# An emission-order model that counts VectorE and GpSimd holding each other up at SBUF

## The chip, the core and the metric

The kernel runs on one core of a Trainium2 chip. The metric is the device time of one execution in microseconds (us); lower is better. TensorE (PE) does matmuls and writes to PSUM, VectorE (DVE), ScalarE (ACT) and GpSimd (POOL) do elementwise work, and SyncE (SP) issues the DMA transfers. Each engine works through its own queue of instructions in the order in which the program wrote them, and semaphores hold an instruction until the data it needs are there.

## The reference

One layer of a latent generator in float32, with 1024 latent tokens and 256 context tokens of width 1024:

```
hn   = rms_norm(h) * gain * (1 + scale) + shift          # h = ctx, then x
proj = hn @ w_in                                          # columns: q,k,v | a,b | z | u_pool | z_pool
q, k, v = silu(short_conv(qkv, 5 taps));  q, k = l2_norm(q), l2_norm(k)
o    = gated_delta_rule(q, k, v, g, beta, state)          # 8 heads, both directions, chunked
o    = rms_norm(o_f + o_b) * silu(z)
y    = (box_mean(u_pool) - u_pool) @ pool_w * silu(z_pool) # 4 groups, windows 2, 4, 8, 16
out  = rms_norm(x + gate * (concat(o, y) @ w_out))
```

The context runs first through the same weights; only its final scan states are used, as the start of the scans of x.

## The kernel before

Matmuls of the large projections are done in three passes of split operands: a weight tile `w` is split into `whi` (ACT copies it, rounded) and `wlo` (POOL subtracts `whi`), an input tile into `hnhi` and `hnlo`, and the products hi*hi, lo*hi and hi*lo are added up in one PSUM bank (`gemm_half`).

The program is written out by Python generators. A **main** generator walks over the tiles of the projections: sixteen context tiles (k and v of each head), then for every head of x the tiles v, k, z and q, some tiles of the pooling branch, and in a second pass the pooling tiles and the output projection. Everything else is a **side thread**: `x_sums` and `inputs` (norm, transposition and splitting of x; `x_half`, `x_split`), `conv_post` (the other four taps of the convolution on DVE, then a tanh on ACT, then one more DVE operation), `thread_a` to `thread_s` (the delta rule of one head after another: `stage_a`, `stage_b`, `stage_q`, `stage_s`, `scan_x`), and later `mix_all`, `pool_out`, `load_all` (pooling) and the loads of the output weights.

Which step is written next is decided by the class `Flow`, a model of the engines' time. Its `free` has for each engine the modelled time at which its queue runs empty. `spend` books an instruction: it starts when its engine is free and its operands are there (plus a fixed delay, `AFTER`), and lasts what `Engine.cost` says. For DVE that is 65 + 1.04 ns per element per partition, and 61 more with a per-partition scalar operand; for a POOL `tensor_tensor` 148 + 2.1 ns per element, and 1040 ns where it raises to a power (`power`). So a `scalar_tensor_tensor` of 128x512 on DVE counts as 658 ns, one of 128x256 as 392 ns, a POOL `tensor_tensor` of 128x512 as 1223 ns and of 128x1024 as 2298 ns.

`run` steps the main generator, and before each of its steps every side thread that is due: `due` is the time at which a thread's last operation is finished by the model or, where the thread names an engine that it wants next, not before that engine's queue is within `SLACK` (500 ns) of running empty. A thread is written as soon as the model's PE time has reached its due time. The thread list is in order of priority, `x_sums` and `inputs` first. Flags (`conv`, `k`, `B`, `done`, `mixed`, `pw` and others) let threads and main wait for one another; a flag bears a modelled time.

So the model's numbers are never seen by the chip. They only set in which order the instructions stand in the five queues: a step which the model takes to be ready early is written early, and its engine then waits at that place in the queue if the chip isn't as far.

At the end of the second pass, `load_all` loads and splits the pooling weights of each group (`pwr`, `pw`, flag `pw`), `mix_all` does the box sums on DVE, and `second_half` releases the pool of tiles `poola` once the flag `mixed` is there and puts the tiles of the output projection in its place.

Of the kernel before, what the change touches and what calls it, by code (L numbers as in the profile page):

```python
# [48 lines left out]
GROUPS = (2, 1, 3, 0)  # L49
# [9 lines left out]
PSUM_TAGS = ("mm", "pp", "pa", "sc", "o")  # L59
# [5 lines left out]
}  # L65
ISSUE = 1220.0
LANDED = 950.0


class Flow:  # L70
# [3 lines left out]
    def __init__(self):  # L74
        self.free = dict(pe=0.0, act=0.0, dve=0.0, pool=0.0, sync=0.0)
        self.dma = 0.0
        self.cur = None
        self.flags = {}
        self.sides = []
        self.seen = {}, {}  # L80
        self.slots = {}
        self.stored = 0.0
        self.banks = [0.0, 0.0]


    def born(self, name, place, bufs):
# [15 lines left out]
    def start(self, eng, uses):  # L102
        t = self.free[eng]
        for name, p0, p1, f0, f1, w in uses:
            for v in (1, 0) if w else (1,):
                for (q0, q1, g0, g1, e), end in self.seen[v].get(name, {}).items():
                    if end + 3000.0 > t and q0 < p1 and p0 < q1 and g0 < f1 and f0 < g1:
                        if e == "sync":
                            d = LANDED + (ISSUE if eng == "sync" else 0.0)
                        elif eng == "sync":  # L110
# [15 lines left out]
                            del old[r]  # L126
            self.seen[w].setdefault(name, {})[p0, p1, f0, f1, eng] = end

    def spend(self, eng, ns, uses):
        start = self.start(eng, uses)  # L130
        end = self.free[eng] = start + ns
        self.note(eng, uses, end)
        t = self.cur
        if t is not None:
            t.next = max(t.next, end + NEXT[eng])
            t.last = eng

    def transfer(self, size, uses, load):
# [3 lines left out]
        self.note("sync", uses, end)  # L142
        self.stored = end + LANDED - ISSUE
        t = self.cur
        if t is not None and load:
            t.next = max(t.next, end + LANDED)
            t.held = True
# [166 lines left out]
class Engine:  # L314
# [46 lines left out]
    def __getattr__(self, op):  # L361
        f = getattr(self.real, op)

        def call(*a, **k):
            self.flow.spend(self.name, self.cost(op, a, k), self.uses(op, a, k))
            return f(*a, **k)  # L366

        return call
# [24 lines left out]
def kernel(  # L393
# [23 lines left out]
    pe, act, dve, pool = (Engine(flow, e, n) for e, n in (  # L417
        (nc.tensor, "pe"), (nc.scalar, "act"), (nc.vector, "dve"), (nc.gpsimd, "pool")))
# [225 lines left out]
    def hnx(b, k, t0):  # L644
# [13 lines left out]
                 u=iter([U0 + i * P for i in CH]),  # L658
# [47 lines left out]
    for i, xt in enumerate(xs):  # L706
        sync.dma_start(out=xt, in_=x_d[:, i, :])
        landed.append(flow.dma + LANDED)
    act.activation(out=wab[:, :, 0, :], in_=wab_r, func=ACTF.Copy)
# [886 lines left out]
    start = [ab_gemm(False), next(ctx), next(ctx)]  # L1596
# [180 lines left out]
    def u_back(n):  # L1777
        if n >= NU:
            yield ("up", CH[n - NU])
        sync.dma_start(out=ups[n % NU][:, :, 8:8 + GW], in_=uscr[n].rearrange("p (r w) -> p r w", w=GW))  # L1780
        flow.settle(flow.dma + LANDED)
        flow.flag("u", n)
# [46 lines left out]
    def out_main():  # L1829
# [6 lines left out]
        def free_raw(slot):  # L1836
            free.append(slot)
            flow.flag("rel", released[0])
            released[0] += 1
# [49 lines left out]
        def y_part(t, hf, k0, k1):  # L1889
            hi, lo = ys[t, hf]  # L1890
            load_split(hi[:, k0:k1], lo[:, k0:k1],
                       yscr[hf * KT + k0:hf * KT + k1, :, t * P:(t + 1) * P].rearrange("k p i -> p k i"),
                       "pool", ("y", t, hf, k0))

        def y_tiles(t, hf, al, bufs):
            ys[t, hf] = [al([P, KT, P], f"y{s}", bufs, FP32R) for s in ("hi", "lo")]
# [69 lines left out]
        def ot2(shape, tag, bufs=1, dtype=FP32):  # L1966
            return pools["c"].tile(shape, dtype, tag=tag, name=tag, bufs=bufs)

        def second_half():
            yield ("mixed",)  # L1970
            pl_p.release()
            pools["c"] = Pool(flow, tc.alloc_tile_pool(name="outc", bufs=1, side="right", reuse_waits="tile"))
            wos = {k: [ot2([P, D], f"wo{s}{n}", 1, FP32R) for s in ("hi", "lo")] for n, k in enumerate(KS[:4])}
            yield ("pool", 2)
            for t in range(2):
                y_tiles(t, 1, ot2, 2)
                y_part(t, 1, *PARTS[0])
                wo_load(KS[t], *wos[KS[t]])
            for k in KS[2:4]:
                wo_load(k, *wos[k])  # L1980
            yield ("pool", 3)
            for slot in ("zp0", "zp1"):
                free_raw(slot)
            for t in range(2):
                y_part(t, 1, *PARTS[1])
            for k in KS[4:]:
                wo_load(k, *[pb([P, D], f"d{s}", 4, FP32R) for s in ("hi", "lo")])
            yield ("wo", KS[5])
            closed.update(("zp0", "zp1", "outb"))
            while not closed.issubset(free):  # L1990
                yield ("rel", released[0])
            cols["gate"], cols["fgain"] = gate, fgain = [pb([P, D], "zp", 2) for _ in range(2)]
            sync.dma_start(out=gate, in_=gate_d.partition_broadcast(P))
            sync.dma_start(out=fgain, in_=final_gain.partition_broadcast(P))
            x_load(0)
            x_load(1)
            yield ("heads",)
            y_tiles(2, 1, oa, 3)
            for p in PARTS:
                y_part(2, 1, *p)  # L2000
            y_load(3, 0, oa, 3)
            y_load(3, 1, oa, 3)
# [80 lines left out]
```

## Time and profile before

| what | value |
|---|---|
| time, median of 3 runs | 1300.84 us (1292.27 to 1300.85) |
| the profiled execution | 1300.56 us |
| its span, first to last instruction | 1298.8 us |
| mean granted TensorE clock | 0.97 |
| PE busy | 1202.6 us (93%) |
| DVE busy | 907.3 us (70%) |
| ACT busy | 582.5 us (45%) |
| POOL busy | 413.9 us (32%) |

"Busy" is the time in which an engine has at least one instruction in work. An idle gap is written in brackets with the instruction that ended it. All instructions have one line, 366, because a helper records them; so tiles, not lines, tell them apart. Tile names are written out<-in.

### The profile page before, as it was taken

What the parts mean: (1) busy time and instruction counts of PE and PEld (TensorE: products, weight loads), DVE (VectorE), ACT (ScalarE), POOL (GpSimd) and SP (SyncE); (2) the same over time, 40 slices, a digit from 0 to 9 for tenths busy, and PEclk for the clock granted to TensorE, in tenths of its full rate; (3) what the DMA queues carried; (4) which work ended last, traced back from release to release, by engine and by line L of the source; (5) the groups of instructions that cost most, each with busy time, mean ns of one, the idle gap of its engine ahead of it and who ended that gap; (6) DMA issues with size and microseconds to landing.
All of it is one profiled execution on the core that took longest, in us unless ns stands there. A gap on an engine that the chain in (4) does not pass through costs nothing.

```text
span 1298.8 us, 26423 instructions
## 1 busy us (share of the span) xinstructions
PE 1202.6 (93%) x10631; PEld 965.7 (74%) x10631; DVE 907.3 (70%) x1867; ACT 582.5 (45%) x1514; POOL 413.9 (32%) x447
## 2 busy tenths in 40 slices
PE   8876799899899999999999999999999989799997
PEld 1675667777787887877778778777788767688886
DVE  4798789778885787788886878887334999624212
ACT  2476637544446547464474464643623223322110
POOL 2466433220411413214142232241315544412330
PEclk9887799999998999999999999999999989899999
DMA  9542254223120313112231132212313135664230
GB/s 324 202 114 81 64 150 142 75 58 91 37 49 18 106 46 103 44 52 77 64 104 29 39 102 62 76 49 50 103 52 120 33 122 183 208 206 148 83 112 33
DMA packets 157384, 123.73 MB, mean 95 GB/s; under 512 B 47106, under 2 KB 135115, under 8 KB 157261
## 3 DMA queue, kind: packets, MB, share of 16 engines
q1 hardware_dynamic: 157261, 122.04, 31.1%
q8 instruction: 83, 1.36, 0.4%
q14 instruction: 40, 0.33, 0.1%
HBM read 101.43 MB, written 20.60 MB: 94 GB/s over the span
## 4 chain that ended last, share of the span: by engine, by line
PE 53%; DVE 31%; ACT 7%; DMA 4%; issue 4%; POOL 2%; SPq 0%; DVEq 0%; POOLq 0%; ACTq 0%
PE mm L366 31%; DVE kT L366 7%; PE sc L366 6%; PE o L366 6%; DVE t L366 6%; PE pp L366 5%; PE pa L366 4%; DVE vT L366 4%; DVE ws L366 3%; ACT junk L366 2%; DVE B L366 1%; DVE qT L366 1%; DVE D L366 1%; ACT u L366 1%; ACT ks L366 1%
## 5 line engine op out<-in xcount | busy, mean ns | idle before, releaser
L366 PE MATMUL mm<-hnhi,wlo 128*128 128x512 f32 x768 | 319.2, 416 | 0.0
L366 PE MATMUL mm<-hnhi,whi 128*128 128x512 f32 x768 | 319.1, 416 | 0.0
L366 PE MATMUL mm<-hnlo,whi 128*128 128x512 f32 x768 | 315.9, 411 | 0.0
L366 POOL TENSOR_TENSOR wlo<-wraw,whi 128x512 fp32r<-128x512 f32 x110 | 156.9, 1432 | 401.0 <-ACT whi L366 391.7
L366 PEld LDWEIGHTS mm<-hnhi,wlo 128*128 128x128 f32 x768 | 146.6, 191 | 24.8 <-issue 0.9
L366 PEld LDWEIGHTS mm<-hnhi,whi 128*128 128x128 f32 x768 | 146.9, 191 | 23.9 <-issue 0.9
L366 PEld LDWEIGHTS mm<-hnlo,whi 128*128 128x128 f32 x768 | 147.0, 191 | 22.8
L366 DVE SCALAR_TENSOR_TENSOR kT<-u,cw,kT 128x512 f32<-128x512 f32 (+1 forms) x96 | 100.9, 1053 | 5.4 <-ACT kT L366 1.8
L366 ACT ACTIVATE y<-sc 128x256 f32<-128x256 f32 (+1 forms) x65 | 25.1, 386 | 126.1 <-PE sc L366 120.8
L366 DVE SCALAR_TENSOR_TENSOR t<-t,laneN 128x1 f32<-128x1 f32 (+4 forms) x150 | 62.3, 415 | 13.2 <-POOL t L366 7.5
L366 ACT ACTIVATE u<-mm 128x512 f32<-128x512 f32 (+1 forms) x64 | 34.6, 541 | 81.4 <-PE mm L366 81.3
L366 DVE SCALAR_TENSOR_TENSOR vT<-u,cw,vT 128x512 f32<-128x512 f32 (+1 forms) x80 | 67.6, 852 | 1.8
L366 ACT ACTIVATE whi<-wraw 128x512 fp32r<-128x512 f32 x110 | 67.4, 631 | 1.9 <-DMA wraw<-in_w_in_dram 1.5
L366 DVE TENSOR_TENSOR pw<-mm,zp 128x512 f32<-128x512 f32 (+1 forms) x12 | 8.0, 669 | 84.3 <-PE mm L366 84.3
L366 ACT ACTIVATE D<-D,ngc 128x128 f32<-128x128 f32 x160 | 53.1, 404 | 25.2 <-POOL D L366 24.9
L366 DVE SCALAR_TENSOR_TENSOR qT<-u,cw,qT 128x512 f32<-128x512 f32 (+1 forms) x80 | 61.0, 768 | 3.8 <-ACT qT L366 2.1
L366 DVE SCALAR_TENSOR_TENSOR S<-S,egl,sc 128x128 f32<-128x128 f32 x112 | 33.7, 342 | 35.6 <-PE sc L366 33.1
L366 DVE SCALAR_TENSOR_TENSOR r<-sc,neg,vn 128x128 f32<-128x128 f32 x128 | 38.7, 344 | 16.7 <-PE sc L366 16.7
L366 DVE SCALAR_TENSOR_TENSOR D<-pp,sm,D 128x128 f32<-128x128 f32 x128 | 35.6, 343 | 20.8 <-PE pp L366 20.7
L366 PEld LDWEIGHTS sc<-r,B 128*128 128x128 f32 x256 | 36.0, 190 | 18.4 <-issue 8.2
L366 PE MATMUL sc<-r,B 128*128 128x128 f32 x256 | 41.0, 283 | 9.4 <-DVE r L366 9.4
L366 PE MATMUL sc<-S,kT 128*128 128x128 f32 x256 | 40.8, 282 | 8.8 <-DVE S L366 8.5
(407 smaller groups left out, 2756.4 us busy)
## 6 DMA issues: line engine op xcount, KB each, us to landing
wraw<-in_w_in_dram SPq DMA_DIRECT2D x55, 512.0 KB, 3.9
D<-gscr SPq DMA_DIRECT2D x40, 256.0 KB, 3.8
qd<-escr SPq DMA_DIRECT2D x16, 512.0 KB
kT<-in_w_in_dram SPq DMA_DIRECT2D x9, 512.0 KB, 3.9
whnhi<-in_w_mod_dram SPq DMA_DIRECT2D x8, 512.0 KB, 3.5
whnlo<-in_w_mod_dram SPq DMA_DIRECT2D x8, 512.0 KB, 9.4
D<-in_w_mod_dram SPq DMA_DIRECT2D x8, 512.0 KB, 3.5
yscr<-zs SPq DMA_DIRECT2D x8, 512.0 KB, 2.9
```

The costliest lines, as they stand in the source:

```text
L366: return f(*a, **k)
```

## The change

`spend` gets a flag `shared`. It is set for each POOL `tensor_tensor` and for each DVE instruction none of whose operands lies in PSUM. For a shared instruction the model looks up the last four shared instructions of the other engine that were booked so far, and adds up the time for which their modelled intervals overlap the new one's. If the new one is DVE's, it is made longer by 0.9 of that; if it is POOL's, DVE's queue is pushed back by 0.9 of it. The intervals themselves and POOL's time are as before. Besides, `second_half` waits for one flag more, `pw` of the last group, before it releases the pool. No instruction is added, removed or given another operand; what can differ is their order.

```diff
+HOLD = 0.9
...
+        self.port = dict(dve=[], pool=[])
...
-    def spend(self, eng, ns, uses):
+    def spend(self, eng, ns, uses, shared=False):
         start = self.start(eng, uses)
-        end = self.free[eng] = start + ns
+        end = start + ns
+        if shared:
+
+            there = self.port["pool" if eng == "dve" else "dve"]
+            both = sum(max(0.0, min(end, b) - max(start, a)) for a, b in there)
+            if eng == "dve":
+                end += HOLD * both
+            else:
+                self.free["dve"] += HOLD * both
+            self.port[eng] = self.port[eng][-3:] + [(start, end)]
+        self.free[eng] = end
         self.note(eng, uses, end)
...
         def call(*a, **k):
-            self.flow.spend(self.name, self.cost(op, a, k), self.uses(op, a, k))
+            u = self.uses(op, a, k)
+            shared = (op == "tensor_tensor" if self.name == "pool" else
+                      self.name == "dve" and not any(v[0].split("_")[0] in PSUM_TAGS for v in u))
+            self.flow.spend(self.name, self.cost(op, a, k), u, shared)
             return f(*a, **k)
...
         def second_half():
             yield ("mixed",)
+            yield ("pw", GROUPS[-1])
             pl_p.release()
```

## Rows read from the trace of the kernel before

**Rows 1.** The page: busy time of PE, and the granted clock of TensorE in 40 equal slices of the span (tenths of full speed).

```profile
PE 1202.6 (93%) x10631; PEld 965.7 (74%) x10631; DVE 907.3 (70%) x1867; ACT 582.5 (45%) x1514; POOL 413.9 (32%) x447
...
PEclk9887799999998999999999999999999989899999
```

**Rows 2.** Busy time by stretch (from:to, length; busy us and instructions of PE, weight loads, DVE, ACT, POOL; granted clock, DMA share, GB/s).

```profile
40.00:110.00 70.00, 54.99 (x351) 48.85 (x349) 61.23 (x99) 45.47 (x105) 42.84 (x63) 0.85 0.43 126
110.00:200.00 90.00, 71.01 (x706) 55.61 (x707) 69.82 (x158) 48.43 (x110) 38.89 (x47) 0.85 0.36 101
...
900.00:1000.00 100.00, 99.06 (x978) 81.83 (x978) 38.51 (x91) 41.84 (x130) 32.78 (x40) 1.00 0.27 89
1000.00:1050.00 50.00, 47.29 (x208) 38.45 (x207) 48.43 (x37) 11.35 (x17) 25.16 (x21) 1.00 0.24 69
1050.00:1100.00 50.00, 43.98 (x182) 35.36 (x181) 46.80 (x60) 14.38 (x21) 20.67 (x9) 0.93 0.47 152
```

**Rows 3.** Who PE waited for over the whole span (us in total, times, longest).

```profile
PE pp L366 <- ACT W L366: 9.5, 3, 8.3
PE sc L366 <- DVE r L366: 9.4, 9, 1.7
PE sc L366 <- DVE S L366: 8.5, 8, 1.7
PE pp L366 <- ACT pw L366: 6.9, 1, 6.9
PE pp L366 <- DVE pw L366: 5.7, 1, 5.7
```

**Rows 4.** Groups of DVE instructions of one shape over the whole span (count | busy us, mean ns of one | idle before).

```profile
L366 DVE SCALAR_TENSOR_TENSOR kT<-u,cw,kT 128x512 f32<-128x512 f32 x64 | 79.3, 1243 | 2.6
...
L366 DVE SCALAR_TENSOR_TENSOR qT<-u,cw,qT 128x512 f32<-128x512 f32 x64 | 48.9, 770 | 1.2
```

**Rows 5.** Timelines (start us, us, engine): one DVE convolution step with no POOL instruction beside it, then one with a POOL `tensor_tensor` beside it, and that one.

```profile
304.27 0.75 DVE L366 SCALAR_TENSOR_TENSOR qT<-u,cw,qT 128x512 f32<-128x512 f32 x1
...
681.16 2.77 DVE L366 SCALAR_TENSOR_TENSOR kT<-u,cw,kT 128x512 f32<-128x512 f32 x1
...
680.54 2.84 POOL L366 TENSOR_TENSOR qd<-qd,qT 128x1024 f32<-128x1024 f32 x1
```

**Rows 6.** Timelines of DVE and POOL: two DVE steps of the triangular inverse, the first beside a POOL `affine_select`.

```profile
716.06 0.64 DVE L366 SCALAR_TENSOR_TENSOR t<-t,laneN 128x36 f32<-128x36 f32 x1
...
716.96 0.25 DVE L366 SCALAR_TENSOR_TENSOR t<-t,laneN 128x49 f32<-128x49 f32 x1
...
715.99 0.64 POOL L366 TENSOR_SCALAR_AFFINE_SELECT D<-D 128x512 f32<-128x512 f32 x1 [0.63 <-DMA D<-gscr]
```

**Rows 7.** The group of DVE's transposes over the whole span, then the timelines of DVE and POOL where four of them stand beside a power on POOL.

```profile
L366 DVE STREAM_TRANSPOSE B<-W 32x256 f32<-32x256 f32 x40 | 17.0, 425 | 0.4
...
574.71 1.74 DVE L366 STREAM_TRANSPOSE B<-W 32x256 f32<-32x256 f32 x4
...
573.68 2.25 POOL L366 TENSOR_TENSOR sm<-sm,expo 128x8 f32<-128x8 f32 x1
```

**Rows 8.** Timelines of DVE, ACT and PE at the end of the context's convolutions.

```profile
114.82 4.27 DVE L366 SCALAR_TENSOR_TENSOR kT<-u,cw,kT 128x256 f32<-128x256 f32 x4
...
121.82 2.10 DVE L366 SCALAR_TENSOR_TENSOR qT<-u,cw,qT 128x256 f32<-128x256 f32 x4
...
119.20 0.42 ACT L366 ACTIVATE u<-kT 128x256 f32<-128x256 f32 x1 [3.41 <-DVE kT L366]
...
124.02 0.42 ACT L366 ACTIVATE u<-qT 128x256 f32<-128x256 f32 x1 [2.60 <-DVE qT L366]
124.34 0.76 ACT L366 ACTIVATE W<-pp,md 128x512 f32<-128x512 f32 x1
...
125.16 1.11 PE L366 MATMUL pp<-ident,B 128*128 128x128 f32 x4 [8.26 <-ACT W L366]
```

**Rows 9.** Timelines of DVE, ACT, POOL and PE in the middle of a head of x.

```profile
590.78 8.06 DVE L366 SCALAR_TENSOR_TENSOR kT<-u,cw,kT 128x512 f32<-128x512 f32 x4
...
598.94 1.06 ACT L366 ACTIVATE u<-kT 128x1024 f32<-128x1024 f32 x1 [2.21 <-DVE kT L366]
...
600.38 2.12 ACT L366 ACTIVATE ks<-pp,sm 128x128 f32<-128x128 f32 x8
...
592.70 5.59 POOL L366 TENSOR_TENSOR qd<-qd,qT 128x1024 f32<-128x1024 f32 x2
...
604.37 0.68 PE L366 MATMUL sc<-r,B 128*128 128x128 f32 x4 [1.66 <-DVE r L366]
```

**Rows 10.** Timelines of DVE, ACT and PE in the pooling stage.

```profile
1055.25 3.76 DVE L366 TENSOR_TENSOR ws<-ws 128x1216 f32<-128x1216 f32 x2
1058.93 0.69 DVE L366 TENSOR_TENSOR pw<-pwr,pw 128x512 fp32r<-128x512 f32 x1
...
1051.63 0.62 ACT L366 ACTIVATE pw<-pwr 128x512 fp32r<-128x512 f32 x1
...
1059.67 1.22 PE L366 MATMUL pp<-dhi,pw 128*128 128x512 f32 x2 [5.67 <-DVE pw L366]
```

**Rows 11.** The SP queue and DVE where the pooling weights of the last group are loaded and split: the first load of the second half's `y`, and the end of the split.

```profile
1119.80 0.39 SPq L384 DMA_DIRECT2D outb<-yscr  x1
...
1124.91 0.68 DVE L366 TENSOR_TENSOR pw<-pwr,pw 128x512 fp32r<-128x512 f32 x1
```

## The prediction

> **What bounds the kernel now.** I read the page first: PE has work in 1202.6 of 1298.8 us [rows 1], so 96 us are all that a better order could give back at PE, plus what the granted clock takes; it is under nine tenths of full speed in 7 of the 40 slices, four of them the second to the fifth [rows 1]. A different order changes neither the matmuls nor their number. The table by stretch tells where the 96 us lie. From 40 to 200 us PE is idle for 34 of 160 us (70 - 54.99 and 90 - 71.01) and the clock is 0.85, and from 40 to 110 DVE is busy for 61.23 of 70 us: DVE, with the convolutions of the context, sets the pace there. Late in the heads of x (900 to 1000) PE is busy for 99.06 of 100 us and sets it itself. From 1000 to 1100 DVE is busy for 95.23 of 100 us, with box sums, and PE loses 8.7 us [rows 2]. The list of PE's waits gives the causes: the largest are a single wait of 8.3 us for `W` within 9.5, the two steps of the scans with 9.4 and 8.5 us in many small pieces, and 6.9 and 5.7 us for `pw` [rows 3]. None of these alone is as much as 1% of the time.
>
> **Whether the model's new number has a ground.** It does. A convolution step of 128x512 takes 0.75 us alone and 2.77 us beside a POOL product of 2.84 us [rows 5]. The same shape has a mean of 770 ns for `qT` and of 1243 ns for `kT` [rows 4]; `kT` is what is in work when POOL multiplies `qd` [rows 9], and 64 x (1243 - 770) ns = 30 us is what `kT` alone loses. The model before counts 658 ns for either.
>
> **What the change corrects, and by how much.** For one such step it adds at most 0.9 x 658 = 592 ns, since the overlap is taken with the step's unhindered interval. The chip added 2.77 - 0.75 = 2.02 us [rows 5]. In a run of steps behind each other the correction repeats as long as the modelled POOL operation lasts: the four `kT` steps that took 8.06 us beside `qd` [rows 9] were 4 x 658 = 2.63 us in the model and become at most 2.63 + 4 x 0.59 = 5.0. At the end of the context, 4.27 + 2.10 us for eight steps of 128x256 [rows 8] were 8 x 392 = 3.1 us and become at most 3.1 + 8 x 0.35 = 5.9 if POOL stood beside all of them, some 4.5 with it beside half. So I take it that about half of the model's lag behind the chip goes where DVE has many shared steps in a row, and next to nothing for lone short steps.
>
> **Part by part, against the profiled execution of 1300.56 us** (span 1298.8 and 1.8 around it; the median of the three runs is 1300.84, so both stand for the same state).
>
> *End of the context (A).* PE waits 8.26 us because ACT takes `W` out of PSUM only at 124.34; it stands behind two tanh (`u<-kT`, `u<-qT`) which wait for DVE for 3.41 and 2.60 us [rows 8]. They were written ahead of `W` because the model had DVE done by then. If the later DVE times put `W` ahead of the last tanh alone, it gains up to the 2.60 us that ACT idles; ahead of both, 2.60 + 3.41 = 6.0. Behind that, eight pieces of the second half of x go through ACT, so what is gained is late no more unless DVE, which also splits half of them, is next. Ends: 0 and 6.0, and a clock at 1.00 instead of 0.85 [rows 2] for the some 14 us of PE work around it would give 2 more; I take 4, since only half the lag goes.
>
> *Heads of x (B).* The stall of 1.66 us at 604.37 has the same form: the tanh of `kT` stands on ACT for 2.21 us waiting for the slowed DVE steps, and eight copies of `ks` (2.12 us) and, behind them, what the scan needs, wait behind it [rows 9]. It is one of the nine pieces of the 9.4 us for `r`. The 8.5 us for `S` [rows 3] hang on lone short steps, which hardly change. Ends: 0 and 9.4 + 8.5 = 17.9; I take 9.4 / 2 = 5, PE being what bounds this stretch, so that a stall avoided there is time won.
>
> *Pooling (C).* `pw` of a group is ready on ACT at 1052.25, but DVE splits it at 1058.93, behind box sums that the model took to be short (two of them 3.76 us), and PE stands for 5.67 us [rows 10]. With longer box sums in the model fewer are written ahead of the split. But DVE has as much to do as before, and the box sums passed over are then late instead: the end of this stretch is DVE's. Ends: 0 and 5.67; I take 2.
>
> *The added wait (D).* `second_half` now steps after the split of the last `pw`. What is queued behind it are the loads of `y` and of the output weights on SP. The first such load already left at 1119.80, and the split ended at 1124.91 + 0.68 [rows 11]; as the wait only moves places in the queues and SP does not itself wait for DVE, the load can leave when it does now. I cost it at nothing; the other end, if these loads came to stand behind something that waits for the split, is 1125.6 - 1119.8 = 5.8 us, hidden as long as PE has products of the first half left.
>
> *What the shuffle costs (E).* Every order after the first altered step is new, and stalls come up where there were none. Nothing in the trace before shows them. It can also win, where a stall that has nothing to do with the ports goes by the way: at best the 6.9 us of the other `pw` [rows 3]. At worst it takes as much as A to C win, 11 us. Between -6.9 and 11 I take 1.5.
>
> Sum: 1300.56 - 4 - 5 - 2 + 0 + 1.5 = **1291** us, 0.7% under the time before. A measurement of this kernel tells about 1%, 13 us, from no change.
>
> **Rivals.** (1) *The correction is too small to matter.* A DVE step that meets a POOL product is held until that is nearly over, whatever its own length: 2.77 us against 2.84 [rows 5], and a step of 36 elements takes 0.64 beside a POOL `affine_select` of 0.64 us, where the next, larger one takes 0.25 [rows 6]; the change gives the first 0.59 instead of 2.02 and does not count `affine_select` at all. Then `W` and the tanh keep their order, and the stalls move by tenths: 1300 us, plus or minus 5. For it: the lone steps ahead of the scans. Against it: in rows 8 and 9 the steps come in rows of four, where the correction adds up. The Trainium skill ("SBUF — State Buffer", section "Who interferes with whom") speaks for this rival: the pair of ports is locked for a whole instruction and the other engine is blocked until its end, rather than slowed by a share; by that rule the correction is of the wrong kind for a single step, and the trace agrees in rows 5.
>
> (2) *More goes than half.* If A and B are put right to their ends, 6 + 2 of clock + 9, and the pooling to 5: 1300.56 - 22 = 1278. For it: PE runs at 0.85 of the clock for 160 us [rows 2], and fewer gaps give some of that back. Against it: 61.23 of 70 us of DVE work in the first stretch don't get fewer by an order.
>
> (3) *Slower: lag invented.* The change also lengthens what does not suffer. Four transposes beside a POOL power take 1.74 us, 435 ns each, against a mean of 425 [rows 7]; the power itself is booked as a shared operation of 1040 ns. One head has such a run of transposes in `stage_a`, and up to 4 x 0.9 x 0.33 = 1.2 us of false lag with it (by the model 65 + 1.04 x 256 = 331 ns each); the reductions of the same chain add about as much. Then the steps that follow are written late and the chain of a head grows by some 2 us: 8 heads x 2 = 16 us, 1317. It decides from the point where PE runs out of projection tiles while `done` of a head is awaited. Against it: PE is busy for 99.06 of 100 us near the end of the heads [rows 2], so the chain has room now.
>
> (4) *It doesn't do what it says*: the order comes out the same, 1300.8. Against it: the overlap is all over the trace [rows 4, 5, 9].
>
> **How the numbers follow.** The forecast 0.45 (own range 1284 to 1298), rival 1 0.18, rival 2 0.19, rival 3 0.15, rival 4 0.03. Faster by over 1% (under 1287.8): all of rival 2 and a third of the forecast, 0.34. Slower by over 1% (over 1313.8): rival 3 and little else, 0.17. Within 1%: 0.49. For 8 in 10 the range has to take in the forecast and rivals 1, 2 and 4 up to the near side of rival 3: 1273 to 1314.
>
> **What would show it.** A right: the gap ahead of the second transposed piece of x's second half under 5 us, and `W` ahead of a tanh on ACT. B right: PE's wait for `r` at about half of 9.4 us, and ACT's idle time ahead of `u<-kT` filled with `ks`. C right: less than 5.67 us for `pw`. D right: the first `y` load of the second half no later against the last `pw` load than now. E is PE's gaps in places where there were none. The prediction is wrong if PE's idle time stays near 96 us (rival 1), falls under 75 (rival 2), or if the heads of x show a wait for `done`, with PE under 90 of 100 us late in the heads (rival 3). DVE's busy time may change by as much as other pairs of operations meet; a large fall there would be a gain that I don't count.

## The result, and the profile after

The changed kernel takes 1308.55 us (median of 19 runs) against 1299.13 us before (19 runs): 1.0065 times as long, with a 95% interval of 1.0039 to 1.0091. Three of the 19 runs of the changed kernel (1317.08, 1318.60 and 2368.10 us) count as slow, and the ratio is that of the means of the other sixteen and of the 19 before. The forecast was 1291 us. The time lies in the range, but on the other side of no change. The profiled execution took 1312.34 us, with a span of 1310.6 us; 11.8 us of span are to be explained.

The page of the changed kernel: PE's busy time, and the granted clock in 40 slices.

```profile
PE 1213.2 (93%) x10631; PEld 977.2 (75%) x10631; DVE 915.2 (70%) x1867; ACT 582.8 (44%) x1514; POOL 410.1 (31%) x447
...
PEclk9898899869999999989999999999998998999999
```

Beside [rows 1]: PE idles for 1310.6 - 1213.2 = 97.4 us, before for 96.2. So 1.2 of the 11.8 us are idle time and 10.6 are busy time, with the same 10631 matmuls: PE worked longer at the lower clock (mean granted clock 0.959, before 0.970). The ninth slice (262 to 295 us) has a 6 where before it had a 9.

Busy time by stretch in the changed kernel (columns as in [rows 2]).

```profile
40.00:110.00 70.00, 54.38 (x357) 48.96 (x356) 61.37 (x97) 49.86 (x115) 47.25 (x68) 0.88 0.42 121
110.00:200.00 90.00, 76.00 (x740) 59.22 (x739) 76.12 (x170) 48.25 (x115) 36.28 (x43) 0.89 0.40 114
260.00:300.00 40.00, 28.95 (x387) 23.59 (x387) 26.14 (x70) 15.22 (x34) 3.39 (x7) 0.70 0.05 10
900.00:1000.00 100.00, 94.03 (x954) 77.60 (x954) 36.40 (x93) 39.47 (x126) 25.58 (x31) 0.97 0.25 77
1000.00:1050.00 50.00, 50.00 (x222) 41.33 (x221) 42.57 (x31) 12.09 (x20) 28.20 (x23) 1.00 0.26 73
1050.00:1100.00 50.00, 45.70 (x198) 36.49 (x196) 47.61 (x61) 12.88 (x18) 20.60 (x13) 1.00 0.46 151
1150.00:1200.00 50.00, 41.96 (x169) 33.02 (x168) 21.03 (x24) 13.87 (x24) 10.87 (x11) 0.93 0.49 164
```

Two of these stretches were not shown of before:

```profile
260.00:300.00 40.00, 39.57 (x412) 32.13 (x411) 30.27 (x86) 15.43 (x34) 9.78 (x14) 1.00 0.27 67
1150.00:1200.00 50.00, 50.00 (x221) 41.17 (x220) 19.46 (x23) 10.63 (x20) 10.04 (x10) 1.00 0.51 160
```

The stretches of the forecast's gains did gain: 110 to 200 us has 5.0 us more PE work than in [rows 2], and 1000 to 1100 us 4.4 us more. New losses stand at 260 to 300 (PE loses 10.6 us, at a clock of 0.70 instead of 1.00), 900 to 1000 (5.0 us) and 1150 to 1200 us (8.0 us).

Who PE waited for in the changed kernel (total, times, longest).

```profile
PE pp L381 <- ACT Y L381: 8.3, 3, 6.0
PE sc L381 <- ACT y L381: 6.4, 7, 1.5
...
PE pp L381 <- DVE VV L381: 5.5, 1, 5.5
...
PE sc L381 <- DVE S L381: 5.0, 8, 1.1
...
PE o L381 <- ACT yhi L381: 4.9, 1, 4.9
PE pp L381 <- ACT ks L381: 4.4, 1, 4.4
...
PE pp L381 <- ACT W L381: 3.0, 2, 1.8
...
PE sc L381 <- DVE r L381: 0.9, 4, 0.3
...
PE pp L381 <- DVE pw L381: 0.2, 1, 0.2
```

Every wait at which the forecast aimed is smaller than in [rows 3]: `W` 9.5 to 3.0, `r` 9.4 to 0.9, `pw` (DVE) 5.7 to 0.2 us. In their place stand `Y`, `y`, `VV`, `yhi` and `ks`.

**Where the time went.** The projection matmuls (those written into `mm`, without the 32 with `scv` at the start) come in the same order in both kernels. Numbered through, each can be matched with itself, and its start in one trace subtracted from that in the other (each number rounded by itself):

| from matmul to matmul | place | starts in before (us) | change in lateness (us) | late by then (us) |
|---|---|---|---|---|
| 0 to 648 | context, first tiles of head 0 | to 249.8 | -15.0 | -15.0 |
| 648 to 744 | head 0 | to 283.6 | +2.2 | -12.8 |
| 744 to 752 | before the `v` tile of head 1 | to 287.4 | +23.9 | +11.0 |
| 752 to 2304 | heads 1 to 7 | to 972.3 | -7.1 | +3.9 |
| 2304 to 2400 | end of the heads | to 998.3 | +8.2 | +12.1 |
| 2400 to 2719 | pooling | to 1096.7 | -14.6 | -2.5 |
| 2719 to the end | output | to 1298.8 | +14.3 | +11.7 |

So the projections were up to 15 us ahead twice and lost it each time, at three places.

Not all of such a lead is time won, since the projections are not PE's only work. By number 648 PE had been idle for 29.6 us instead of 37.5, which is 7.9 of the 15.0 us. The other 6.9 are busy time: 228 of PE's other products, which before stand ahead of this place, were still to come, and the clock was 0.91 instead of 0.89. Between 744 and 752 PE does these products (16.6 us busy, before 3.7) and is idle for 11.0 us. The pooling and the output are like that too: in the pooling PE has 8.6 us less of idle and 5.9 us less of busy time, in the output 6.8 and 7.4 us more.

### The profile page after: what moved, and what is told of

Read it like the earlier page. It is cut to its first block, busy times and chain, and to the rows that moved or that the text cites. A ratio compares the mean times of both kernels' runs of the same rounds, so it can differ in the third digit from the quotient of the medians.

```text
span 1310.6 us, 26416 instructions
## 1 busy us (share of the span) xinstructions
PE 1213.2 (93%) x10631; PEld 977.2 (75%) x10631; DVE 915.2 (70%) x1867; ACT 582.8 (44%) x1514; POOL 410.1 (31%) x447
## 4 chain that ended last, share of the span: by engine, by line
PE 60%; DVE 17%; ACT 8%; DMA 6%; issue 4%; POOL 3%; SPq 0%; DVEq 0%; POOLq 0%; ACTq 0%
PE mm L381 38%; PE pp L381 6%; PE o L381 6%; PE sc L381 5%; PE pa L381 4%; DVE kT L381 4%; DVE t L381 3%; ACT junk L381 2%; DVE qT L381 2%; DMA wraw<-yscr 1%; DVE B L381 1%; DVE vT L381 1%; DMA D<-gscr 1%; DMA wraw<-in_w_out_dram 1%; POOL wlo L381 1%
## 5 line engine op out<-in xcount | busy, mean ns | idle before, releaser
L381 DVE SCALAR_TENSOR_TENSOR kT<-u,cw,kT 128x512 f32<-128x512 f32 (+1 forms) x96 | 93.5, 980 | 5.0 <-ACT kT L381 1.8
L381 DVE SCALAR_TENSOR_TENSOR r<-sc,neg,vn 128x128 f32<-128x128 f32 x128 | 38.7, 345 | 23.7 <-PE sc L381 23.5
L381 POOL TENSOR_SCALAR_AFFINE_SELECT D<-D 128x512 f32<-128x512 f32 x40 | 32.8, 822 | 65.7 <-DMA D<-gscr 65.7
L381 DVE SCALAR_TENSOR_TENSOR D<-pp,sm,D 128x128 f32<-128x128 f32 x128 | 35.7, 343 | 23.9 <-PE pp L381 23.8
L381 PEld LDWEIGHTS sc<-S,kT 128*128 128x128 f32 x256 | 36.6, 192 | 13.5 <-issue 9.1
L381 POOL TENSOR_TENSOR ylo<-wraw,yhi 128x1024 fp32r<-128x1024 f32 (+2 forms) x9 | 19.4, 2151 | 87.2 <-ACT yhi L381 82.4
```

## The experiments

Each ratio is to the kernel before, with its 95% interval. The two right columns are changes in lateness as in the table above: ahead of the `v` tile of head 1 (744 to 752) and at the end of the heads (2304 to 2400), from each kernel's profiled execution. The two columns ahead of them are what the emission model itself says: for how long, by its own clock, its main generator waits there for the flag `v` of head 0 and for `done` of head 7 (0 stands for under 1.5 us; the expectations call the model the planner). e15 and e16 stand in the text.

One execution has some scatter: the change, e2 and e4 have the same order up to the end of the heads, and there their projections are 12.1, 17.2 and 9.4 us late. The changes at the two places agree better, within 3 us at 744 and 0.4 us at 2304.

| kernel | ratio | interval | model: `v` 0 | model: `done` 7 | at 744 | at 2304 |
|---|---|---|---|---|---|---|
| the change | 1.0065 | 1.0039 to 1.0091 | 21.1 | 8.0 | +23.9 | +8.2 |
| e1 wait only | 0.9995 | 0.9982 to 1.0008 | 0 | 4.2 | 0.0 | 0.0 |
| e2 first pass | 1.0080 | 1.0056 to 1.0105 | 21.1 | 8.0 | +26.7 | +8.3 |
| e3 second pass | 1.0013 | 1.0000 to 1.0025 | 0 | 4.2 | 0.0 | 0.0 |
| e4 no wait | 1.0074 | 1.0050 to 1.0098 | 21.1 | 8.0 | +23.9 | +7.9 |
| e5 until the context's end | 1.0019 | 1.0002 to 1.0037 | 0 | 4.2 | -0.7 | 0.0 |
| e6 until head 0 | 1.0074 | 1.0047 to 1.0102 | 21.1 | 4.2 | +23.4 | 0.0 |
| e7 from head 0 | 1.0048 | 1.0020 to 1.0076 | 0 | 8.0 | 0.0 | +8.5 |
| e8 pairs only | 1.0112 | 1.0084 to 1.0140 | 0 | 8.0 | -0.6 | +8.5 |
| e9 factor -0.3 | 1.0386 | 1.0369 to 1.0403 | 0 | 16.5 | -0.6 | +18.8 |
| e10 factor 0.05 | 1.0145 | 1.0124 to 1.0165 | 0 | 16.5 | 0.0 | +19.3 |
| e11 lock | 1.0325 | 1.0296 to 1.0354 | 17.4 | 16.5 | +16.5 | +19.2 |
| e12 slack 480 | 1.0072 | 1.0046 to 1.0099 | 0 | 8.0 | 0.0 | +7.6 |
| e13 delay 270 | 0.9992 | 0.9970 to 1.0014 | 0 | 4.2 | 0.0 | 0.0 |
| e14 slack 520 | 1.0072 | 1.0043 to 1.0100 | 0 | 4.2 | -0.6 | 0.0 |
| e17 change, delay 270 | 1.0114 | 1.0074 to 1.0154 | 21.1 | 16.5 | +23.9 | +19.3 |
| e18 change, delay 250 | 1.0072 | 1.0039 to 1.0105 | 21.1 | 8.0 | +23.9 | +7.7 |

**The change taken apart (e1 to e4).** Two theories stood against each other: that the loss arises in the heads' half, and that it arises in the output, where the lateness grew by 14.3 us last.

e1, the wait alone:

```diff
-HOLD = 0.9
+HOLD = 0.0
```

> The added wait for the last pw flag, without the longer DVE times (the factor is 0). In the written order only the last few DMA issues on SP and two or three DVE steps of the tail stand elsewhere than before. Theory (step D of the prediction: the wait costs nothing): 1300 us, ratio to before 0.998 to 1.002. Rival (the wait holds back the loads of the second half's y, which in the changed kernel left 13.7 us later, 1133.51 against 1119.80): 4 to 8 us more, ratio 1.003 to 1.006, with PE's stall at the last y load longer than before.

0.9995: the added wait costs nothing that shows (the interval ends at 1.0008).

e2, the factor in the first half alone:

```diff
-                end += HOLD * both
+                end += self.hold * both
...
     flow.run(main())
     flow.drain()
+    flow.hold = 0.0
...
-            yield ("pw", GROUPS[-1])
```

> The factor 0.9 only while the context and the heads are written; the pooling and the output are booked as before, and the added wait is left out. Theory 1 (the loss arises in the heads' half: matched matmuls of the projections are 12.1 us later than before where the heads end, and what the pooling gave back belongs to the other half's order): 1308 to 1313 us, ratio 1.006 to 1.010. Theory 2 (the loss arises in the tail, where the changed kernel loses 14 us between the last projection matmul and the end): 1298 to 1302 us, because the 12 us at the end of the heads come back in the pooling, which is bound by DVE and had time to spare; ratio 0.998 to 1.002.

1.0080, with the projections 17.1 us late from the end of the heads to the last one, and 17.0 at the end of the span. (Its profiled execution, 1317.62 us, is the slowest of its ten; their median is 1310.72.) The theory of the output fell: lateness from the heads isn't taken up by the pooling when its order is that of before.

e3, the factor in the second half alone, with the wait:

```diff
+        self.hold = 0.0
...
     flow.run(main())
     flow.drain()
+    flow.hold = HOLD
```

> The factor is 0 while the context and the heads are written and 0.9 from the pooling on, with the added wait. Theory 1 (the loss arises in the heads' half): no wait for pw of 5.67 us, a lost 14 us in the tail against 14.6 us won in the pooling: 1297 to 1301 us, ratio 0.997 to 1.001. Theory 2 (the loss arises in the tail): 1308 to 1314 us, ratio 1.006 to 1.011, with the y loads of the second half issued some 10 us later than before.

1.0013. The last projection matmul starts 14.9 us earlier than before, and the end is 1.2 us later. Why, shows in DVE's last step of the pooling in e3:

```profile
1138.47 0.74 DVE L382 SCALAR_TENSOR_TENSOR zp<-pp,psc,zp 128x512 f32<-128x512 f32 x1
```

and the same in before, where PE was 14.9 us later:

```profile
1138.71 0.74 DVE L366 SCALAR_TENSOR_TENSOR zp<-pp,psc,zp 128x512 f32<-128x512 f32 x1
```

It doesn't move. In e3 it stands behind a split of output weights (`wolo`), which waits for ACT's copy, and that for a load:

```profile
1136.23 1.06 ACT L382 ACTIVATE wohi<-wraw 128x1024 fp32r<-128x1024 f32 x1 [2.83 <-DMA wraw<-in_w_out_dram]
...
1137.32 1.23 DVE L382 TENSOR_TENSOR wolo<-wraw,wohi 128x1024 fp32r<-128x1024 f32 x1 [2.00 <-ACT wohi L382]
```

and so it does in before:

```profile
1136.48 1.06 ACT L366 ACTIVATE wohi<-wraw 128x1024 fp32r<-128x1024 f32 x1 [1.84 <-DMA wraw<-in_w_out_dram]
...
1137.57 1.23 DVE L366 TENSOR_TENSOR wolo<-wraw,wohi 128x1024 fp32r<-128x1024 f32 x1 [0.90 <-ACT wohi L366]
```

What comes of the step is stored, loaded again as `y` and split, and in e3 PE stands for it:

```profile
1164.87 0.79 PE L382 MATMUL o<-wohi,yhi 128*128 128x512 f32 x1 [7.07 <-ACT yhi L382]
```

From 1000 to 1110 us the pooling is DVE's (busy for 105.19 of 110 us in before, 106.37 in e3); from there to this step DVE waits for the loads of the output weights (in before twice for PE too, 2.17 and 2.69 us). PE's 14.9 us turn into 9.2 us more of idle time behind the last projection (23.6 instead of 14.4), most of it for `yhi`, and 6.9 us more of busy time, with 12 products put off to there and a clock of 0.96 instead of 0.98.

e4, the change without the wait:

```diff
-            yield ("pw", GROUPS[-1])
```

> The changed kernel without the added wait; two issues on SP and one DVE step stand elsewhere than in the changed kernel, all other queues are the same. Theory (the wait costs nothing): as the changed kernel, 1306 to 1311 us, ratio to before 1.005 to 1.009. Rival (the wait makes the tail late): 1298 to 1304 us, ratio 0.999 to 1.003.

1.0074, as the change. With e1, the wait is out of the question from both sides.

**The first half taken apart (e5 to e8).** The factor is switched by a flag (`self.hold` in the place of `HOLD`, as in e2). e5 drops it when the last convolution of the context is written:

```diff
     def flag(self, *name):
+        if name == ("k", -1):
+            self.hold = 0.0
```

> The factor 0.9 only until the last context convolution is written (the flag that lets the second context job start); all later bookings, and the end of the program, are as before, without the added wait. Theory (the loss is one place, 260 to 300 us, where PE stands for the v of head 0, because the delta-rule chain of the context and head 0 was written later; the gain at the end of the context is real and is kept): the gap of 8.26 us for W is gone, no wait of over 3 us for VV, ratio 0.988 to 0.997. Rival 1 (the gain at the end of the context is given back whatever is done later, since the chain of head 0 sets when main can go on): 0.998 to 1.003. Rival 2 (the chain is made late by the context's own new order): 1.004 to 1.010.

1.0019: rival 1. The wait for `W` falls from 9.5 to 3.0 us, PE is idle for 4.4 us less by number 648, and the projections are 6.2 us ahead there. But between 752 and 864, at the tiles of head 1, they lose 9.6 us, and they are 1.4 us late at the end of the heads. (e5 and e6 keep the added wait, other than their expectations say; by e1 it costs nothing that shows.)

e6 drops it at `("v", 0)` instead:

```diff
+        if name == ("v", 0):
+            self.hold = 0.0
```

> The factor 0.9 until the v of head 0 is written as ready, that is over the whole stretch up to 300 us; the other heads, the pooling and the output are booked as before, without the added wait. Theory (the loss is this stretch): as the first pass alone, ratio 1.004 to 1.010, with PE busy for about 29 of 40 us from 260 to 300 us at a clock of 0.7. Rival (the loss comes from the later heads): 0.996 to 1.002.

1.0074: the loss of the whole change is there with the order of the context and head 0 alone.

What PE does there in the changed kernel:

```profile
278.37 0.26 PE L381 MATMUL pp<-Y,B 32*32 32x32 f32 x1 [2.82 <-ACT B L381]
...
284.98 2.42 PE L381 MATMUL pp<-VV,B 64*64 64x64 f32 x32 [5.54 <-DVE VV L381]
...
292.90 1.11 PE L381 MATMUL pa<-ident,vT 128*128 128x128 f32 x4
295.30 0.66 PE L381 MATMUL pa<-ident,vT 128*128 128x128 f32 x4 [1.29 <-ACT vn L381]
```

and the last two in before:

```profile
277.65 0.60 PE L366 MATMUL pa<-ident,vT 128*128 128x128 f32 x4
...
280.07 0.66 PE L366 MATMUL pa<-ident,vT 128*128 128x128 f32 x4
```

Only when `vT` of head 0 has been transposed can the `v` tile of head 1 take its place (`v_tile` waits for the flag `v` of the head before). In before that is at 280.07, and the tile starts at 287.4 without a wait. In the changed kernel it is at 295.30; the projections, 12.8 us ahead, have nothing to go on with, and PE does the chain's small matmuls with idle time between them. The chain itself got late on its way, as DMA issues on SP show. In before, the first store of a triangular step (`ds`) of the second context job, its result (`vs`), and the first store of head 0:

```profile
208.55 0.37 SPq L384 DMA_DIRECT2D ds<-t  x1
...
233.69 0.32 SPq L384 DMA_DIRECT2D vs<-t  x1
...
277.93 0.36 SPq L384 DMA_DIRECT2D ds<-t  x1
```

and in the changed kernel:

```profile
211.55 0.37 SPq L399 DMA_DIRECT2D ds<-t  x1
...
243.86 0.57 SPq L399 DMA_DIRECT2D vs<-t  x1
...
291.76 0.36 SPq L399 DMA_DIRECT2D ds<-t  x1
```

3.0, 10.2 and 13.8 us later, while the projections were up to 15 us earlier.

e7 sets the factor at `("v", 0)` and drops it at the end of the heads:

```diff
+        if name == ("v", 0):
+            self.hold = HOLD
...
     flow.run(main())
     flow.drain()
+    flow.hold = 0.0
```

> The factor 0.9 only from the v of head 0 to the end of the heads; everything else as before, without the added wait. Theory (the loss is the stretch before): ratio 0.996 to 1.002, the wait for r under 3 us instead of 9.4 us, and the 8 us so won spread over other waits. If step B of the prediction were right in its size, 0.994 to 0.997. Rival (the heads lose, some 2 us each): 1.006 to 1.012.

1.0048, neither theory's number, with an interval that reaches into both. With e6 the two parts would come to 1.2%, and the change costs 0.65%: the losses don't add up. The waits of e7:

```profile
PE pa L384 <- DVE kT L384: 7.3, 5, 2.2
PE sc L384 <- ACT y L384: 6.7, 8, 1.6
...
PE pp L384 <- ACT ks L384: 4.3, 1, 4.3
...
PE sc L384 <- DVE r L384: 1.4, 4, 0.7
```

Two of these in before:

```profile
PE pa L366 <- DVE kT L366: 4.6, 2, 3.6
...
PE sc L366 <- ACT y L366: 0.9, 1, 0.9
```

`r` is down from 9.4 to 1.4 us, but `y` and `kT` are up: from number 752 to 2304 PE is idle for 29.1 us, before for 29.3. The projections are 3.1 us ahead at number 2304, with 20 of PE's other products put off (652.4 us busy, before 655.6). Then they run out: the last head's chain isn't done, and PE stands for `ks`. In before it doesn't:

```profile
981.72 2.14 PE L366 MATMUL pp<-ident,ks 128*128 128x128 f32 x8
```

in the change it does:

```profile
992.15 2.29 PE L381 MATMUL pp<-ident,ks 128*128 128x128 f32 x8 [4.36 <-ACT ks L381]
```

e8 counts fewer operations as shared:

```diff
-            shared = (op == "tensor_tensor" if self.name == "pool" else
-                      self.name == "dve" and not any(...))
+            shared = (op == "tensor_tensor" and k.get("op") != ALU.pow if self.name == "pool" else
+                      self.name == "dve" and op in ("tensor_tensor", "scalar_tensor_tensor")
+                      and not any(...))
```

> The whole change with the factor 0.9, but only DVE operations with two tensors from SBUF and POOL products count as shared; transposes, reductions, copies and POOL powers no longer do. Theory (invented lag, rival 3 of the prediction, makes the chain late): ratio 0.993 to 1.002, and PE busy for over 36 of 40 us from 260 to 300 us. Rival (any longer DVE time makes the chain late, whether the chip has it or not): 1.004 to 1.012.

1.0112. Taking out what does not suffer makes it no better. The other sign of the theory did come: PE is busy for 37.60 of the 40 us from 260 to 300, and nothing is lost at 744. But at number 864 the projections are 12.0 us late, the change's 4.9. So invented lag may be what makes the chain late at `v` of head 0; without it the order loses as much elsewhere.

**The lag or the deal (e9 to e12).** Is it the booked lag that costs, or does any other order cost (a new deal: any booked time that differs puts other steps first)?

```diff
-HOLD = 0.9
+HOLD = -0.3
```

> The changed kernel with the factor -0.3 in place of 0.9: a DVE step beside a POOL product is booked as shorter, the wrong way. Theory 1 (steps booked as late are written late and make the chain of the heads longer; the sign counts): ratio 0.994 to 1.001. Theory 2 (the kernel before is one good order among many, and any other costs): 1.002 to 1.012.

```diff
-HOLD = 0.9
+HOLD = 0.05
```

> The changed kernel with the factor 0.05: the modelled times hardly differ (at most 33 ns for one step of 128x512), but the order does. Theory 1 (the size of the booked lag counts): ratio 0.998 to 1.002. Theory 2 (any other order costs): 1.002 to 1.012.

```diff
-                end += HOLD * both
+                for a, b in there:
+                    if a < end and start < b:
+                        end = max(end, b)
```

> The changed kernel, but a shared DVE step that meets a POOL product is booked to end no earlier than the product, which is nearer to the 2.77 us beside 2.84 us of the trace than 0.9 of the overlap. Theory 1 (booked lag makes the chain late, and the more of it the more): ratio 1.008 to 1.025. Theory 2 (any other order costs about the same): 1.002 to 1.012. Rival (rival 1 of the prediction: with a correction of the right kind the order would win): 0.985 to 0.998.

```diff
-SLACK = 500.0
+SLACK = 480.0
```

> The kernel before with one constant changed that has nothing to do with the ports: a thread may name its step 480 instead of 500 ns ahead of the moment at which the engine's queue runs empty. No DVE time is booked longer. Theory 1 (booked lag costs): ratio 0.997 to 1.002. Theory 2 (any other order costs): 1.002 to 1.012.

1.0386, 1.0145, 1.0325 and 1.0072; the first three lie above every range that I had given. A factor of 0.05 costs twice as much as 0.9, and 20 ns in a constant that has nothing to do with the ports cost as much as the change. The lag alone can't be it. A correction nearer to what the trace shows of single steps (e11) is far worse, though it isn't a clean one: it holds transposes and reductions too, counts powers as products, and keeps the 0.9 on POOL's side. e10 at the end of the heads:

```profile
995.01 2.28 PE L381 MATMUL pp<-ident,ks 128*128 128x128 f32 x8 [5.57 <-ACT ks L381]
```

The lateness there comes in three sizes in all kernels of the table, 0, about 8 and about 19 us, with waits for `ks` of under 0.3, 4.35 and 5.57 us; and the model's own wait for `done` tells which (4.2, 8.0, 16.5 us).

**Neutral deals, and cover for the last head (e13 to e16).** e13 and e14 deal the order anew and leave the model's wait at 4.2 us:

```diff
-    ("dve", "pe"): 260.0
+    ("dve", "pe"): 270.0
```

> The kernel before with one constant of the planner changed, the delay from DVE to PE, 270 instead of 260 ns; a good tenth of DVE's queue stands elsewhere, and the planner's wait for the last head stays at 4.2 us as before. Theory (what costs is the end of the heads, and orders which leave that alone are as good as before): ratio 0.998 to 1.003, no wait of over 2 us for ks at the end of the heads. Rival (any other order costs): 1.005 to 1.015.

```diff
-SLACK = 500.0
+SLACK = 520.0
```

> The kernel before with the other neutral constant raised, 520 instead of 500 ns; a fifth of DVE's queue stands elsewhere; the planner's wait for the last head stays at 4.2 us. Theory (end of the heads): ratio 0.997 to 1.003, no wait of over 2 us for ks there. Rival (any other order costs): 1.005 to 1.015.

0.9992 and 1.0072. Both keep the end of the heads, as the model's wait told, but e14 loses 9.8 us earlier, between matmuls 752 and 864, at the tiles of head 1; there e5 lost 9.6 us, and e8 and e9 lose 11.2 and 11.4. So the end of the heads is one place of several. The model tells the neutral deals apart: by its own clock main comes to its last output tile 0.7 us later than in before in e13, 5.5 us in e14 and 11.1 us in e12.

e15 and e16 put a projection tile behind the last head, e15 in the change and e16 in the kernel of e1:

```diff
-END = ""
+END = "u"
```

> The changed kernel with one u tile of the pooling moved to the end of the first half, behind the last head; its result goes through DRAM, as for the tiles that were already early. Theory (the end of the heads is where the change loses): PE's wait of 4.36 us for ks there is gone and the matched matmuls are some 8 us earlier at that place; if the pooling and the output take it over, ratio to before 0.998 to 1.003, against 1.0065 of the change. Rival (the loss is spread over the heads, or the output's second half sets the end anyway): 1.005 to 1.010.

> The same tile moved in the kernel before (with the added wait, which alone cost nothing). There is no wait for ks at the end of the heads to remove. Theory (end of the heads): 0.997 to 1.003, so that e15 and this one come out alike. Rival (the tile wins by itself, through less DVE work that is late in the pooling): 0.988 to 0.996.

1.0095 (1.0059 to 1.0132) and 1.0078 (1.0052 to 1.0104). In e15 the lateness at the end of the heads grows by 0.9 instead of 8.2 us, as intended, and the time doesn't follow: the last projection is 1.3 us early and the end 9.8 us late, so that the output loses 11.1. The tile isn't a remedy; e16, which has no such wait to lose, is 0.8% slower with it, above both of its ranges.

**The same deal in the changed kernel (e17, e18).** The delay of e13, up and down, with the factor at 0.9:

```diff
-    ("dve", "pe"): 260.0
+    ("dve", "pe"): 270.0
```

> The changed kernel with the delay from DVE to PE at 270 instead of 260 ns, as in e13. The planner's own wait at the end of the heads is 16.5 us instead of 8.0. Theory (the deal behind head 0 decides, and the planner's wait tells the loss at the end of the heads): a wait of 5.57 us for ks there, the projections some 19 us behind instead of 8, ratio to before 1.010 to 1.018. Rival (the loss is the change's own): as the change, 1.004 to 1.009.

> The changed kernel with that delay at 250 ns. The planner's wait at the end of the heads stays at 8.0 us. Both theories: a wait of 4.35 us for ks, ratio 1.004 to 1.010; a spread beyond that (under 1.002 or over 1.012) speaks for the deal of the order in the heads between.

1.0114 and 1.0072. In e17 the heads end as its model said, with 5.58 us for `ks` and 19.3 us more lateness. But its projections were 12.7 us ahead by then (the change's 3.9 us late), so that they are only 6.6 us late behind it, less than the change's 12.1. Its profiled execution is the second fastest of its six, and the interval of the ratio reaches down into the change's: that e17 is slower than the change is not shown.

## Why the prediction was wrong

**What bounds the kernel.** This is the reading that failed. From "PE is busy for 99.06 of 100 us late in the heads" [rows 2] I took it that PE sets the pace there. But main's projections fill whatever time the chain of the heads leaves, so a busy PE only says that there were projections left. The chain (DVE, ACT and DMA from one head to the next) sets when `v` of head 0 and `done` of head 7 come; DVE and then the loads of the output weights set when the last `y` comes. PE's stalls in between move the projections, not these.

**A (taken at -4).** Its place was right and its size, up to there, about right: `W` fell from 9.5 to 3.0 us, and by number 648 PE was idle for 7.9 us less (4.4 in e5, where it stands alone). The sign that I named didn't come: a gap of 6.00 us stands at 121.11, at the next transposed pieces. ACT writes `Y`, which PE awaits there, only at 120.28, behind a tanh that waited 2.00 us for DVE and after 2.05 us of its own for POOL's split:

```profile
117.81 0.42 ACT L381 ACTIVATE u<-qT 128x256 f32<-128x256 f32 x1 [2.00 <-DVE qT L381]
120.28 0.78 ACT L381 ACTIVATE Y<-pp,md 128x512 f32<-128x512 f32 x1 [2.05 <-POOL hnlo L381]
```

(The piece at 125.16 in before [rows 8] belongs to the first half of x, not to the second as I had it; it reads `B`, the second half `ks` and `qd`.) The step that failed is "what is gained is late no more": all of it is given back, at `v` of head 0 in the change and at the tiles of head 1 in e5. Its worth is +0.19% in e5 instead of -0.3%.

**B (-5).** `r` fell to 0.9 us, more than the half forecast. "A stall avoided there is time won" is the sentence that failed: in e7, with `r` at 1.4 us, PE's idle time in the heads is 29.1 us instead of 29.3, since other stalls came in its place, and with the wait for `ks` come 8.5 us of lateness at the end of the heads. The worth is +0.48% instead of -0.4%.

**C (-2).** The 5.67 us for `pw` [rows 10] went to 0.2. The reason that I gave against it, "the end of this stretch is DVE's", gave the right outcome: DVE's last step stands at 1138.47 instead of 1138.71 us (held by the loads of the output weights, which I had not seen), and the worth is 0 (e3, 1.0013), not 2.

**D (0).** Right: 0.9995 (e1). The sign that I named is missed by 1.3 us (the first `y` load of the second half leaves 3.1 us behind the last load for `pw`, before 1.8 us), and the time shows nothing of it. It isn't the wait's either: without it (e4) the distance is 3.1 us too, and with it alone (e1) 1.7.

**E (+1.5).** The term that I sized wrong. Four deals with no lag to speak of (e10, e12, e13, e14) cost +1.45, +0.72, -0.08 and +0.72%; their median of 0.72% is 9.4 us. With A to C at nothing and E at 9.4 the sum is 1300.56 + 9.4 = 1310 us, and 1308.55 was measured. As the four spread from -1 to +19 us, that it comes so near is luck. I had bounded E at 11 us by the stalls that A to C remove, which e10 exceeds, and its price lies in places that had hardly a stall before [rows 3], since before happens to pass them in time.

**The signs.** PE's idle time stayed near 96 us (97.4), which I had named as the sign of rival 1; here gains and new stalls cancel in it. PE's 94.03 of 100 us late in the heads are not the under 90 of rival 3, yet the wait of its kind came.

**Rivals.** Rival 1 is out: the order changed everywhere, and the correction nearer to its kind costs 3.3% (e11). That is no evidence against the rule of the Trainium skill ("SBUF — State Buffer", "Who interferes with whom") that I named with it: the model's bookings are not what the chip does. Rival 2's local gains all came, up to their ends, and its time did not. Rival 3 had the point from which it decides, PE out of projections while a head's chain is awaited, and a mechanism that at best explains one place: without the invented lag the stall at `v` of head 0 is gone and the time is 1.0112 all the same (e8). I spread its 16 us over eight heads; they fall on two places, 23.9 and 8.2 us, against the gains of A and B. The reason that I held against it, the busy PE of [rows 2], is the failed reading once more.

**What stays open.** Whether the booked lag costs anything beyond a new deal: kernels with a factor of 0.9 or a part of it lie at 1.001 to 1.011, neutral deals at 0.999 to 1.015, and these can't be told apart with so few. Why the second context job's triangular step became longer is not settled: DVE wrote other threads' steps between its own, but which of them mattered wasn't tried; e8 points at the invented lag and doesn't prove it, since its order differs everywhere. Nor was the 3.9% of e9 followed.

## What to carry to other kernels

Where one engine's long stream of filler work is written around a chain of dependent steps, a full engine doesn't say that it sets the time: look for the flags at which the filler must wait for the chain, and count a stall avoided as nothing if such a flag comes behind it. Add up the idle time of a whole stretch, and the work left over at its end, before a shorter wait is called a gain: in e7 a wait 8 us shorter left the idle time of the heads as it was. The emission model's own list of waits names two of the places, and which of them costs more, and can be read ahead of any run. Before an improvement of a planner is judged by its time, deal the order anew with a neutral constant a few times; here that alone moved the time by -0.1 to +1.5%, more than the effect that was looked for.

## What the runs showed of the hardware

The loss is hardly idle time. Main matmuls of the changed kernel ahead of and behind a rise of the clock:

```profile
265.92 0.63 PE L381 MATMUL mm<-hnhi,whi 128*128 128x512 f32 x1
266.35 0.63 PE L381 MATMUL mm<-hnlo,whi 128*128 128x512 f32 x1
...
267.36 0.39 PE L381 MATMUL mm<-hnlo,whi 128*128 128x512 f32 x1
267.59 0.40 PE L381 MATMUL mm<-hnhi,wlo 128*128 128x512 f32 x1
```

They start 0.43 us apart at the lower level (1.2 GHz) and 0.23 us apart at the upper (2.4 GHz). PE had run such matmuls back to back since 262.3 us; until then small products of 32x16 stood between them. PE was busy with the same matmuls for 10.6 us longer than before, and the stretch from 260 to 300 us, with its gaps, had a mean granted clock of 0.70. So the idle time doesn't tell what an order costs: the change's grew by 1.2 us and its span by 11.8.

Over the whole trace of before, 66 `scalar_tensor_tensor` steps with SBUF operands met POOL products, and nothing else on POOL, for 61.6 us and lasted 38.7 us longer than their unhindered median, 0.63 of the overlap. Of the 38.7 us, 36.6 fall to the 40 steps that began while the product was in work, and 2.1 to the 26 that had begun before it (10.1 us of overlap). So "held until that is nearly over", as rival 1 had it, does not go for steps that begin first. The change takes 0.9 of the overlap of the unhindered step, which is 28.7 us for these 66, and in these terms the trace's factor is 1.35: the 0.9 is too small. Eight steps that met a POOL power for 3.3 us lasted no longer, so counting powers is off too. Neither e8 nor e11 made the order faster; a run with both put right was not made.
